# Two-layer hybrid trunk on one core: the delta layer in two phases with a paced MLP filler, and the rotary's sine product read from the PSUM bank

## The chip, the cores and the metric

One core of a Trainium2 chip. The metric is the device time of one launch in microseconds, on the slowest core; there is one core here. The matmuls run on TensorE (PE), elementwise work on VectorE (DVE), ScalarE (ACT) and GpSimd (POOL), and SyncE (SP) issues the DMAs.

## The reference

Two pre-RMSNorm residual layers over an input of 1024 tokens by 1024 channels, each followed by a squared-ReLU MLP of hidden width 4096, and a final RMSNorm:

```python
for layer in range(2):
    hn = rmsnorm(h, mix_norm[layer])
    h = h + (sparse_pool_mixer if layer % 2 == 0 else gated_deltanet)(hn, ...)
    h = h + square(relu(rmsnorm(h, mlp_norm[layer]) @ w_ff1[layer])) @ w_ff2[layer]
return rmsnorm(h, final_norm)
```

The even layer's mixer projects to queries, keys, an indexer and pooling channels. The indexer picks 256 causal keys a query, eight heads attend to them, and a multi-scale pooling branch stands beside. Queries (8 heads of 64 channels) and index queries (8 of 64) get rotary positions: `[x1 cos - x2 sin, x1 sin + x2 cos]` for the two halves of each head. The odd layer's mixer is gated DeltaNet: 8 heads of 128 channels, a short convolution on q, k and v, a decay for each head, and a delta rule whose state passes from chunk to chunk:

```python
v_new = val - kcd @ state
o = qd @ state + at @ v_new
state = state * gl + kd.T @ v_new
```

`val` and `kcd` need the inverse of a unit lower triangular matrix for each chunk. The inverse has no one matmul; it is built level by level.

## The kernel before, in words

The residual stream lives in SBUF in two halves of 512 tokens, `self.h[0]` and `self.h[1]`, each as eight tiles of 128 channels by 512 tokens. All wide matmuls are in split precision: every operand is a high part and a rest, and `mm3` (L245, L246, L247) issues three matmuls of 128x128 by 128x512 for one product. So the three lines always appear in equal number. `split` makes high part (a copy on ScalarE, L165) and rest (a subtraction on POOL, or on VectorE, L169). Weights come by DMA from SP in a prefetch of fixed order (`prefetch`, L200) into a ring `raw` of 4, and go through the same split into the rings W (6) and WM (4).

The odd layer's order is written by generators that the loop in `odd_heads` (L1123) steps in turn:

- `odd_project` projects one of q, k, v, z of a head (24 wide matmuls in bank `ps_g`), copies it out on ScalarE (L947) and convolves on VectorE (L949).
- `odd_head` (L977) is one delta head as a generator of short steps. Small matmuls build the inverse: L1044 and L1050 each issue 16 of 32x32 by 32x16 at every one of four levels (64 a head in the code, which the trace counts as 128); L1037, L1047 and L1053 are VectorE's parts between them. Then the state chain runs over four chunks: L1088 (state times k), L1089 on VectorE, L1090, a copy on ScalarE, L1093 and L1094 for the output, L1097 and L1101 for the new state. L1074 and L1116 stand between the two parts and at the end. Up to three heads are in flight, a new one every `STAGGER` = 8 steps.
- `output` accumulates two finished heads' share of the output projection into h (`accumulate`, L816 to L841).
- The filler is a half of an MLP (`mlp_half`): wide matmuls of known length that depend on nothing in the heads. In every step of the loop it gets a budget in us, `FILL[above]`: 5.6 for the first filler, 4.7 for the second.

The loop runs over all 16 pairs of half and head in one sequence. The first filler is MLP 1 of the second half ("below"). The second ("above") is MLP 2 of the first half; it may start only when the first half's outputs are all written, which is after the second half's first heads have begun:

```python
if not above and fill is None and written[0] == NH // 2:
    fill, due, above = fills[1](), 0.0, True
if fill:
    due += FILL[above]
```

Before the loop, the first half's norm (`norm_stages`, L312: squares, a root on VectorE at L269, transposes at L276 and L288, then the normed x into ring X) and the projections of two heads run beside the filler. After the loop, the rest of the second filler runs beside the second half's last norm, and the last half MLP runs alone ("alone").

In the even layer, `swapped` (L502 to L509) takes a projected pair of heads from bank `ps_g`: a copy on ScalarE into a tile of ring A, and four DMAs on SP that swap the halves of each head (L508). One step later `query_stacks` (L350) calls `rotate` (L334): cosine product on POOL (L339), sine product on VectorE from the swapped copy (L340), sum on VectorE (L341). The keys go through `rotate` with both operands in PSUM. `even_index` and `even_query` are its users: eight times for the index, eight for the queries.

Of the kernel before, what the change touches and what calls it, by code (L numbers as in the profile page):

```python
# [18 lines left out]
OP = mybir.AluOpType  # L19
# [15 lines left out]
FILL = (5.6, 4.7)  # L35
# [89 lines left out]
class Trunk:  # L125
# [224 lines left out]
    def query_stacks(self, p, s, ring):  # L350

        nc = self.nc
        r = self.rotate(*p, s)
# [100 lines left out]
    def even_latent(self, s, ps):  # L454
# [17 lines left out]
        self.kst.append(self.key_stacks(self.rotate(p1, p2, s, True), self.KS))  # L472
# [8 lines left out]
    def even_index_keys(self, s, ps):  # L481
# [9 lines left out]
        self.kis.append(self.key_stacks(self.rotate(p1, p2, s, True), self.KI))  # L491
# [10 lines left out]
    def swapped(self, ps):  # L502

        pc = self.A.get()
        self.copy(pc, ps)
        ps2 = self.A.get()
        for at in range(0, P, 32):
            self.nc.sync.dma_start(ps2[at:at + 32], pc[at ^ 32:(at ^ 32) + 32])  # L508
        return pc, ps2  # L509

    def even_index(self, s, p, ps):

        pc = self.swapped(ps)
# [43 lines left out]
    def even_query(self, s, p, ps):  # L557

        pc = self.swapped(ps)
# [563 lines left out]
    def odd_heads(self, fills):  # L1123


        seq = [(s, h) for s in range(2) for h in range(NH)]
        x, G, qkvz, ys = [[], []], [None, None], {}, {}
        outs, written = deque(), [0, 0]

        def project(i):  # L1130
            s, h = seq[i]
            if h == 0 and s == 1:
                yield from self.norm_stages(self.h[s], R_MIX + 8, x[s])
                yield
            t = []
            for n in range(4):
                while self.live == self.Q.n:
                    yield
                t.append(self.odd_project(s, h, n, x[s]))
                yield  # L1140
                if h == 0 and n == 1:
                    G[s] = self.odd_gates(x[s], self.grow)
                    yield
            qkvz[i] = t
# [8 lines left out]
        def head(i):  # L1153
            s, h = seq[i]
            yield from self.odd_head(s, h, *qkvz.pop(i), G[s], ys)
# [3 lines left out]
        def step(gen):  # L1159
            return next(gen, self) is not self  # L1160

        self.live = 0
        norm = self.norm_stages(self.h[0], R_MIX + 8, x[0])
        ahead, nxt, fill, due, above = None, 2, fills[0](), 0.0, False
        for n in (4, 2, 2):
            next(norm, None)
            for _ in range(n):
                next(fill)
        for _ in chain(project(0), project(1)):
            next(fill)  # L1170
        active, started, done, age = [], 0, 0, 0
        while done < len(seq) or outs:
            if started in qkvz and (not active or (len(active) < 3 and age >= STAGGER)):
                active.append(head(started))
                started, age = started + 1, 0
            age += 1
            for g in list(active):
                if not step(g):
                    active.remove(g)
                    done += 1  # L1180
            for _ in range(2):
                if outs and not step(outs[0]):
                    outs.popleft()
            if not above and fill is None and written[0] == NH // 2:
                fill, due, above = fills[1](), 0.0, True
            if fill:
                due += FILL[above]
                while fill and due > 0:
                    t = next(fill, None)
                    if t is None:  # L1190
                        fill = None
                    else:
                        due -= t
            if ahead is None and nxt < len(seq) and nxt < done + 3:
                if seq[nxt] == (1, 0) and fill:
                    for _ in fill:
                        pass
                    fill = None
                ahead, nxt = project(nxt), nxt + 1
            if ahead and not step(ahead):  # L1200
                ahead = None
# [29 lines left out]
    def even(self):  # L1231
# [3 lines left out]
        with ExitStack() as st:  # L1235
# [3 lines left out]
            self.Q, self.A = Ring(ep, "q", 4, 1024), Ring(ep, "at", 4, 512)  # L1239
# [154 lines left out]
    def run(self):  # L1394
# [10 lines left out]
        XB = Ring(self.pool("second"), "xb", 8, 1024)  # L1405
# [13 lines left out]

        def above():  # L1420
            xa = []
            for _ in self.norm_stages(self.h[0], R_MLP + 8, xa, XB):
                yield FILL[1]
            yield from self.mlp_half(1, 0, xa, [self.Y])

        fill, x = self.odd([below, above]), []
        for _ in self.norm_stages(self.h[1], R_MLP + 8, x):
# [66 lines left out]
```

## Time and profile before

| what | us |
|---|---|
| three runs | 2773.43, 2786.07, 2784.98 |
| their median | 2784.98 |
| the profiled execution's own time | 2783.84 |
| its span in the profile | 2782.1 |
| TensorE busy in it | 2653.8 (95%) |

All readings below are of that one execution. "Granted clock" (PEclk) is the share of TensorE's full 2.4 GHz that it got; 0.5 is its lower level, 1.2 GHz. The stages on the time axis: even layer 0 to 420 (its attention of the second half, and the start of MLP 1, reach beyond it), MLP 1 of the first half to 840, entry of the odd layer 840 to 1000, its heads to 2310, exit to 2450, the last half MLP alone until the end.

### The profile page before, as it was taken

Reading aid. Unit: us, or ns where it says so; the run is one execution under the profiler, and the core shown is the slowest. Engines: PE = TensorE matmul, PEld = TensorE weight load, DVE = VectorE, ACT = ScalarE, POOL = GpSimd, SP = SyncE. Lnnn points to the kernel's source line nnn. Section 1 sums busy time; section 2 is a strip of 40 time slices with the busy share of each in tenths; the row PEclk is TensorE's granted clock in tenths of the full one; section 3 lists DMA queues with packets and bytes.
Section 4 is the critical chain, followed back from the end, with each engine's and each line's share of the span. In section 5 each row is a group of like instructions: output and inputs, shape, how many; then the busy total and the mean of one; then the engine's idle time right before and its main releaser. Section 6 shows DMA issues by size and latency. Waiting matters only on the chain. (4 is left out here: it accounts for less than half of the span.)

```text
span 2782.1 us, 44603 instructions
## 1 busy us (share of the span) xinstructions
PE 2653.8 (95%) x16640; PEld 2094.9 (75%) x16640; DVE 1660.1 (60%) x3587; ACT 1185.8 (43%) x2480; POOL 1227.5 (44%) x1062
## 2 busy tenths in 40 slices
PE   8789989999999999999999999999999999899998
PEld 6566768787777787777777767777777777688886
DVE  5788998734435655655565777655556645633334
ACT  4557767334444543433333344433334333433332
POOL 4653354542245444434454444434444434544442
PEclk9999989999999999999999999999999999999999
DMA  5221223331123222222222212122222222333332
GB/s 192 76 75 35 68 81 98 91 91 54 42 76 96 80 84 73 80 77 78 68 88 73 62 47 64 59 65 77 75 71 73 69 69 87 118 98 95 96 98 76
DMA packets 121068, 220.91 MB, mean 79 GB/s; under 512 B 14098, under 2 KB 15250, under 8 KB 120850
## 3 DMA queue, kind: packets, MB, share of 16 engines
q1 hardware_dynamic: 120850, 218.05, 25.4%
q8 instruction: 131, 2.15, 0.3%
q14 instruction: 87, 0.71, 0.1%
HBM read 209.61 MB, written 4.19 MB: 77 GB/s over the span
## 5 line engine op out<-in xcount | busy, mean ns | idle before, releaser
L169 POOL TENSOR_TENSOR wm<-raw,wm 128x512 fp32r<-128x512 f32 x425 | 562.0, 1323 | 853.9 <-ACT wm L165 840.3
L165 ACT ACTIVATE wm<-raw 128x512 fp32r<-128x512 f32 x425 | 267.3, 629 | 606.2 <-PE ps_g L246 270.7
L169 POOL TENSOR_TENSOR w<-raw,w 128x512 fp32r<-128x512 f32 x222 | 296.7, 1337 | 351.3 <-ACT w L165 330.8
L841 DVE TENSOR_TENSOR h<-ps_d,h 128x512 f32<-128x512 f32 x392 | 267.1, 685 | 134.4 <-PE ps_d L247 132.4
L245 PE MATMUL ps_g<-x,w 128*128 128x512 f32 x644 | 259.5, 403 | 12.1 <-ACT w L165 9.1
L827 DVE SCALAR_TENSOR_TENSOR ps_g<-ps_g,temps 128x512 f32<-128x512 f32 x128 | 89.1, 696 | 291.0 <-ACT temps L825 291.0
L246 PE MATMUL ps_g<-x,w 128*128 128x512 f32 x644 | 257.1, 399 | 4.3 <-DVE x L380 4.1
L247 PE MATMUL ps_g<-x,w 128*128 128x512 f32 x644 | 256.6, 398 | 1.0 <-POOL w L169 1.0
L245 PE MATMUL ps_d<-y,wm 128*128 128x512 f32 x596 | 243.7, 409 | 10.3 <-DVE h L841 8.7
L165 ACT ACTIVATE w<-raw 128x512 fp32r<-128x512 f32 x222 | 139.0, 627 | 258.3 <-PE ps_g L246 180.9
L247 PE MATMUL ps_d<-y,wm 128*128 128x512 f32 x596 | 236.5, 397 | 0.3 <-POOL wm L169 0.2
L246 PE MATMUL ps_d<-y,wm 128*128 128x512 f32 x596 | 236.0, 396 | 0.0
L245 PE MATMUL ps_g<-xb,wm 128*128 128x512 f32 x512 | 207.7, 406 | 5.6 <-ACT qkvz L947 5.0
L247 PE MATMUL ps_g<-xb,wm 128*128 128x512 f32 x512 | 206.4, 403 | 5.5 <-POOL wm L169 5.4
L246 PE MATMUL ps_g<-xb,wm 128*128 128x512 f32 x512 | 205.7, 402 | 0.0
L949 DVE SCALAR_TENSOR_TENSOR qkvz<-temps,conv,qkvz 128x512 f32<-128x512 f32 x144 | 130.8, 909 | 97.9 <-ACT qkvz L947 96.8
L245 PEld LDWEIGHTS ps_g<-x,w 128*128 128x128 f32 x644 | 123.2, 191 | 40.6 <-ACT w L165 9.9
L245 PE MATMUL ps_g<-x,wm 128*128 128x512 f32 x352 | 141.5, 402 | 7.7 <-ACT wm L165 2.9
L246 PEld LDWEIGHTS ps_g<-x,w 128*128 128x128 f32 x644 | 123.0, 191 | 33.3 <-DVE x L380 6.6
L245 PEld LDWEIGHTS ps_d<-y,wm 128*128 128x128 f32 x596 | 112.0, 188 | 44.9 <-DVE h L841 16.9
L246 PE MATMUL ps_g<-x,wm 128*128 128x512 f32 x352 | 140.9, 400 | 4.4 <-DVE x L169 4.4
L247 PE MATMUL ps_g<-x,wm 128*128 128x512 f32 x352 | 141.1, 401 | 3.2 <-POOL wm L169 3.2
(445 smaller groups left out, 6089.5 us busy)
## 6 DMA issues: line engine op xcount, KB each, us to landing
raw<-in_w_dram SPq DMA_DIRECT2D x456, 256.0 KB, 2.7
raw<-in_woi_dram SPq DMA_DIRECT2D x128, 256.0 KB, 2.6
raw<-in_w2q_dram SPq DMA_DIRECT2D x56, 256.0 KB, 2.6
raw<-in_wei_dram SPq DMA_DIRECT2D x52, 256.0 KB, 2.7
raw<-in_weo_dram SPq DMA_DIRECT2D x32, 256.0 KB, 2.7
raw<-in_woo_dram SPq DMA_DIRECT2D x32, 256.0 KB, 2.7
h<-in_xt_dram SPq DMA_DIRECT2D x16, 256.0 KB, 3.0
at<-at SPq DMA_DIRECT2D x64, 64.0 KB, 2.0
```

The source lines that it names most:

```text
L165: self.nc.scalar.activation(out, in_, AF.Copy)
L169: eng.tensor_tensor(lo, full, hi.bitcast(F32), op=OP.subtract)
L245: mm(ps, wh, xh, start=start, stop=False)
L246: mm(ps, wh, xl, start=False, stop=False)
L247: mm(ps, wl, xh, start=False, stop=stop)
L827: nc.vector.scalar_tensor_tensor(ps, ps, 0.0, r, op0=OP.max, op1=OP.mult)
L841: nc.vector.tensor_tensor(h, ps, h, op=OP.add)
L949: nc.vector.scalar_tensor_tensor(acc, pin[:, j:j + 512], cw(j), acc, op0=OP.mult, op1=OP.add)
```

## The change

Two edits. In the odd layer, the sequence of 16 becomes a loop over the halves: each half has its norm, its first projection, its eight heads and its outputs. In every step the filler gets 3.5 us, or 2.8 where a projection is under way. When the first half's outputs are written, the first half's norm for MLP 2 and what is left of the first filler are issued, then MLP 2 of the first half becomes the filler. The normed x of the second half goes to ring XB, that of the first half's MLP 2 to ring X.

In the even layer, `swapped` becomes `rotated`: VectorE multiplies the bank with the sines before the swap, POOL multiplies the copy with the cosines, the DMAs swap the sine product, and one subtraction (L354) ends it. Ring A gets 6 buffers in place of 4. The functions above the change keep their line numbers up to 353; behind, a line's number is higher by 1 to 8 (L340 stays for the keys; L1044 is L1052 now).

```diff
-FILL = (5.6, 4.7)
+FILL = (3.5, 2.8)
...
-    def rotate(self, p, ps2, s, p_in_psum=False):
+    def rotate(self, p, ps2, s):
...
-        (nc.vector if p_in_psum else nc.gpsimd).tensor_tensor(t1, p, cos, op=OP.mult)
+        nc.vector.tensor_tensor(t1, p, cos, op=OP.mult)
...
     def query_stacks(self, p, s, ring):
...
-        r = self.rotate(*p, s)
+        r, m = p
+        nc.vector.tensor_tensor(r, r, m, op=OP.subtract)
...
-    def swapped(self, ps):
-
-        pc = self.A.get()
+    def rotated(self, ps, s):
...
+        pc, pm = self.A.get(), self.A.get()
+        nc.vector.tensor_tensor(pm, ps, sin, op=OP.mult)
         self.copy(pc, ps)
-        ps2 = self.A.get()
+        nc.gpsimd.tensor_tensor(pc, pc, cos, op=OP.mult)
+        m = self.A.get()
         for at in range(0, P, 32):
-            self.nc.sync.dma_start(ps2[at:at + 32], pc[at ^ 32:(at ^ 32) + 32])
-        return pc, ps2
+            nc.sync.dma_start(m[at:at + 32], pm[at ^ 32:(at ^ 32) + 32])
+        return pc, m
...
+        def filled(us):
+
+            self.due += us
+            while self.due > 0:
+                self.due -= next(fill, 1e9)
...
+        for s in range(2):
+            self.due, G = 0.0, {}
+            norm = self.norm_stages(self.h[s], R_MIX + 8, xs[s], (self.X, self.XB)[s])
+            for n in (4, 2, 2):
+                next(norm, None)
+                for _ in range(n):
+                    next(fill)
+            for _ in project(s, 0, G):
                 next(fill)
...
+            active, started, done, age, ahead, nxt = [], 0, 0, 0, None, 1
+            while done < NH or outs:
...
+                filled(FILL[ahead is not None])
+                if ahead is None and nxt < NH and nxt < done + 3:
+                    ahead, nxt = project(s, nxt, G), nxt + 1
+                if ahead and not step(ahead):
+                    ahead = None
+            if s == 0:
+                xa = []
+                norm = self.norm_stages(self.h[0], R_MLP + 8, xa)
+                for _ in range(3):
+                    next(norm, None)
+                    for _ in range(4):
+                        next(fill, None)
+                for _ in fill:
+                    pass
+                fill = fills[1](xa)
...
-            self.Q, self.A = Ring(ep, "q", 4, 1024), Ring(ep, "at", 4, 512)
+            self.Q, self.A = Ring(ep, "q", 4, 1024), Ring(ep, "at", 6, 512)
...
-        for _ in self.norm_stages(self.h[1], R_MLP + 8, x):
+        for _ in self.norm_stages(self.h[1], R_MLP + 8, x, XB):
```

TensorE in the middle of a head of the second half, where before no filler is left. Before (L1088 to L1097 are the state chain of one head, L1044 and L1050 the inverse of the next, L245 to L247 a projection into `ps_g`):

```order
L1088 MATMUL ps_t<-state,qkvz 128x128
L1093 MATMUL ps_o<-state,qkvz 128x128
L1044 MATMUL ps_t<-xxc,lm 32x16 x12
L1090 MATMUL ps_t<-vb,xx_7987 128x128
L1044 MATMUL ps_t<-xxc,lm 32x16 x4
L247 MATMUL ps_g<-x,w 128x512
L245 MATMUL ps_g<-x,w 128x512
L1094 MATMUL ps_o<-vn,at 128x128
L1097 MATMUL ps_t<-vn,kd 128x128
L1050 MATMUL ps_t<-dy,xtc 32x16 x16
L246 MATMUL ps_g<-x,w 128x512
```

After, the same steps of a head (L1096 to L1105, L1052 and L1058 are the same lines of code):

```order
L1096 MATMUL ps_t<-state,qkvz 128x128
L1101 MATMUL ps_o<-state,qkvz 128x128
L1052 MATMUL ps_t<-xxc,lm 32x16 x12
L1098 MATMUL ps_t<-vb,xx_7971 128x128
L1052 MATMUL ps_t<-xxc,lm 32x16 x4
L245 MATMUL ps_d<-y,wm 128x512
L246 MATMUL ps_d<-y,wm 128x512
L1102 MATMUL ps_o<-vn,at 128x128
L1105 MATMUL ps_t<-vn,kd 128x128
L1058 MATMUL ps_t<-dy,xtc 32x16 x16
L247 MATMUL ps_d<-y,wm 128x512
```

The wide matmuls between the chain's steps are as many as before; they come from the filler (`ps_d`, from `y` and `wm`) where they came from a projection.

VectorE in the first half's projections of the even layer, between the index scores (L545 and L547, now L553 and L555; into score tiles named h_...) and the pooling branch (its bank read is L573, now L581). Before:

```order
L547 SCALAR_TENSOR_TENSOR h_606<-ps_t,wi,h_606 128x384
L545 TENSOR_SCALAR h_617<-ps_t,wi 128x512
L547 SCALAR_TENSOR_TENSOR h_617<-ps_t,wi,h_617 128x512
L573 TENSOR_TENSOR temps<-ps_g,rb 128x512
L575 COPY uhist<-temps 128x16
L547 SCALAR_TENSOR_TENSOR h_606<-ps_t,wi,h_606 128x384
L585 SCALAR_TENSOR_TENSOR h_681<-temps 128x512
L547 SCALAR_TENSOR_TENSOR h_606<-ps_t,wi,h_606 128x384
L587 TENSOR_TENSOR h_681<-temps,ce 128x16
L547 SCALAR_TENSOR_TENSOR h_617<-ps_t,wi,h_617 128x512
L588 TENSOR_TENSOR h_681<-h_681,temps 128x16
L340 TENSOR_TENSOR temps<-at,rope 128x512
```

After:

```order
L354 TENSOR_TENSOR at<-at 128x512
L511 TENSOR_TENSOR at<-ps_g,rope 128x512 x2
L553 TENSOR_SCALAR h_610<-ps_t,wi 128x384
L354 TENSOR_TENSOR at<-at 128x512
L555 SCALAR_TENSOR_TENSOR h_610<-ps_t,wi,h_610 128x384
L553 TENSOR_SCALAR h_621<-ps_t,wi 128x512
L555 SCALAR_TENSOR_TENSOR h_621<-ps_t,wi,h_621 128x512
L354 TENSOR_TENSOR at<-at 128x512
L581 TENSOR_TENSOR temps<-ps_g,rb 128x512
L555 SCALAR_TENSOR_TENSOR h_610<-ps_t,wi,h_610 128x384
L583 COPY uhist<-temps 128x16
L593 SCALAR_TENSOR_TENSOR h_681<-temps 128x512
```

The sine product (L340) stood behind the pooling branch's first rows; now the products (L511) stand further ahead, and the last subtraction (L354) stands before the bank read.

SP in the second half's query projections, the last four swaps of the even layer (L508, now L516) among weight loads (L200). Before:

```order
L508 DMA at<-at 32x512 x4
L200 DMA raw<-in_weo_dram 128x512 x2
L508 DMA at<-at 32x512 x4
L200 DMA raw<-in_w_dram 128x512 x2
L508 DMA at<-at 32x512 x4
L200 DMA raw<-in_w_dram 128x512 x2
L508 DMA at<-at 32x512 x4
L200 DMA raw<-in_w_dram 128x512 x4
```

After:

```order
L516 DMA at<-at 32x512 x4
L200 DMA raw<-in_weo_dram 128x512 x2
L516 DMA at<-at 32x512 x4
L200 DMA raw<-in_w_dram 128x512 x3
L516 DMA at<-at 32x512 x4
L200 DMA raw<-in_w_dram 128x512 x2
L516 DMA at<-at 32x512 x4
L200 DMA raw<-in_w_dram 128x512 x3
```

Two or three loads stand between two swaps, where it was two; one more stands ahead of the third.

## Rows read from the trace of the kernel before

**Rows 1.** The page: busy us, share of the span and number of instructions of each engine.

```profile
PE 2653.8 (95%) x16640; PEld 2094.9 (75%) x16640; DVE 1660.1 (60%) x3587; ACT 1185.8 (43%) x2480; POOL 1227.5 (44%) x1062
```

**Rows 2.** The view by stages, all engines: stretch, its length, then busy us and instructions of PE, PEld, DVE, ACT and POOL, granted clock, DMA share, GB/s.

```profile
140.00:420.00 280.00, 248.30 (x1143) 184.37 (x1144) 248.21 (x576) 185.74 (x382) 122.77 (x89) 0.93 0.21 66
...
1540.00:1770.00 230.00, 211.39 (x2032) 160.85 (x2031) 167.24 (x412) 98.97 (x253) 93.40 (x94) 0.95 0.18 54
...
2450.00:2740.00 290.00, 290.00 (x1265) 237.33 (x1264) 102.43 (x157) 95.50 (x158) 134.72 (x104) 1.00 0.32 96
```

**Rows 3.** The same view for line L245 alone, one of the three wide matmul lines: stretch, length, busy us (count), clock, DMA share, GB/s.

```profile
840.00:1000.00 160.00, 85.27 (x214) 0.99 0.28 88
1000.00:1540.00 540.00, 251.27 (x622) 0.99 0.25 77
1540.00:1770.00 230.00, 81.52 (x193) 0.95 0.18 54
1770.00:1860.00 90.00, 39.63 (x97) 0.96 0.23 72
1860.00:2250.00 390.00, 173.35 (x427) 1.00 0.23 71
2250.00:2310.00 60.00, 27.94 (x70) 1.00 0.26 80
2310.00:2450.00 140.00, 71.15 (x182) 1.00 0.33 104
```

**Rows 4.** The same for line L1044, the inverse's matmuls, 128 in the trace for each head.

```profile
1000.00:1540.00 540.00, 11.50 (x768) 0.99 0.25 77
1540.00:1770.00 230.00, 7.97 (x512) 0.95 0.18 54
1770.00:1860.00 90.00, 1.98 (x128) 0.96 0.23 72
1860.00:2250.00 390.00, 9.52 (x608) 1.00 0.23 71
2250.00:2310.00 60.00, 0.44 (x32) 1.00 0.26 80
```

**Rows 5.** TensorE's waits in the exit, 2310 to 2450: who waited, for what, us in total, times, longest.

```profile
PE ps_g L247 <- POOL wm L169: 2.1, 2, 1.5
PE ps_d L245 <- DVE h L841: 2.1, 3, 1.0
...
PE ps_t L276 <- DVE rs_y L269: 1.1, 1, 1.1
```

**Rows 6.** TensorE's waits in 1540 to 1770.

```profile
PE ps_t L276 <- DVE rs_y L269: 4.0, 2, 2.6
PE ps_t L1044 <- DVE xxc L1037: 2.6, 1, 2.6
PE ps_t L1090 <- DVE vb L1089: 2.4, 3, 1.7
PE ps_o L1094 <- ACT vn L165: 2.1, 2, 1.8
```

**Rows 7.** TensorE's waits in 1000 to 1540, the two largest.

```profile
PE ps_g L245 <- ACT qkvz L947: 3.0, 3, 1.0
PE ps_d L245 <- DVE h L841: 2.3, 5, 0.5
```

**Rows 8.** TensorE's waits in the entry, 840 to 1000.

```profile
PE ps_t L276 <- DVE rs_y L269: 2.6, 1, 2.6
```

**Rows 9.** Groups of VectorE by line and form in the even layer, 0 to 420: count, busy us, mean ns, idle before.

```profile
L341 DVE TENSOR_TENSOR temps<-temps 128x512 f32<-128x512 f32 x20 | 19.8, 992 | 0.4
L340 DVE TENSOR_TENSOR temps<-at,rope 128x512 f32<-128x512 f32 x16 | 16.7, 1046 | 9.2 <-DMA at<-at 9.1
...
L340 DVE TENSOR_TENSOR temps<-ps_t,rope 128x512 f32<-128x512 f32 x4 | 2.8, 690 | 1.2 <-PE ps_t L490 1.0 <-PE ps_t L471 0.2
```

**Rows 10.** Line L340 over the whole span: durations in ns, least, median and longest, first and last start.

```profile
L340 DVE TENSOR_TENSOR temps<-at,rope x16: 677/690/1785, 51.4 to 397.0; 128x512 f32<-128x512 f32 x16
L340 DVE TENSOR_TENSOR temps<-ps_t,rope x4: 681/692/693, 42.5 to 175.0; 128x512 f32<-128x512 f32 x4
```

**Rows 11.** The group of the SBUF form of L340 in 140 to 420.

```profile
L340 DVE TENSOR_TENSOR temps<-at,rope 128x512 f32<-128x512 f32 x9 | 9.4, 1046 | 0.0
```

**Rows 12.** TensorE's waits in 350 to 420.

```profile
PE ps_g L246 <- DVE x L169: 4.4, 2, 3.6
PE ps_g L245 <- ACT wm L165: 2.9, 1, 2.9
```

**Rows 13.** The timeline of VectorE from 383 to 392: start, us, line, operation.

```profile
383.40 1.78 DVE L340 TENSOR_TENSOR temps<-at,rope 128x512 f32<-128x512 f32 x1
...
386.81 1.76 DVE L341 TENSOR_TENSOR temps<-temps 128x512 f32<-128x512 f32 x1
388.49 1.76 DVE L340 TENSOR_TENSOR temps<-at,rope 128x512 f32<-128x512 f32 x1
```

**Rows 14.** VectorE's waits in 0 to 140, the first.

```profile
DVE temps L340 <- DMA at<-at: 9.1, 2, 7.8
```

More of the change, by code (lines that the diff above doesn't have):

```diff
@@ L471, in even_latent @@
         nc.tensor.matmul(p2, self.wkv[:, 128:256], cf, start=True, stop=True)
-        self.kst.append(self.key_stacks(self.rotate(p1, p2, s, True), self.KS))
+        self.kst.append(self.key_stacks(self.rotate(p1, p2, s), self.KS))
         pv = self.bank()
@@ L557, in even_query @@
     def even_query(self, s, p, ps):
-        pc = self.swapped(ps)
+        pc = self.rotated(ps, s)
         yield
@@ L1123, in odd_heads, with step @@
     def odd_heads(self, fills):
[L1126 to L1144, printed above, removed]
+        xs, fill = [[], []], fills[0]()
+        qkvz, ys, outs, written = {}, {}, deque(), [0, 0]
+        def step(gen):
+            return next(gen, self) is not self
         def output(s, h):
@@ L1151, in output, with head @@
             written[s] += 1
-        def head(i):
-            s, h = seq[i]
-            yield from self.odd_head(s, h, *qkvz.pop(i), G[s], ys)
+        def head(s, h, G):
+            yield from self.odd_head(s, h, *qkvz.pop(h), G, ys)
             if h % 2:
                 outs.append(output(s, h))
-        def step(gen):
-            return next(gen, self) is not self
-        self.live = 0
-        norm = self.norm_stages(self.h[0], R_MIX + 8, x[0])
-        ahead, nxt, fill, due, above = None, 2, fills[0](), 0.0, False
@@ L1165, in odd_heads @@
-        for n in (4, 2, 2):
-            next(norm, None)
-            for _ in range(n):
-                next(fill)
[L1169 to L1201, printed above, removed]
@@ new lines, in project @@
+        def project(s, h, G):
+            t = []
+            for n in range(4):
+                while self.live == self.Q.n:
+                    yield
+                t.append(self.odd_project(s, h, n, xs[s]))
+                yield
+                if h == 0 and n == 1:
+                    G.update(self.odd_gates(xs[s], self.grow))
+                    yield
+            qkvz[h] = t
+        def filled(us):
+            self.due += us
+            while self.due > 0:
+                self.due -= next(fill, 1e9)
@@ new lines, in odd_heads @@
+        self.live = 0
+        for s in range(2):
[6 more added lines that the diff above has]
+            for _ in project(s, 0, G):
+                next(fill)
+            active, started, done, age, ahead, nxt = [], 0, 0, 0, None, 1
+            while done < NH or outs:
+                if started in qkvz and (not active or (len(active) < 3 and age >= STAGGER)):
+                    active.append(head(s, started, G))
+                    started, age = started + 1, 0
+                age += 1
+                for g in list(active):
+                    if not step(g):
+                        active.remove(g)
+                        done += 1
+                for _ in range(2):
+                    if outs and not step(outs[0]):
+                        outs.popleft()
+                filled(FILL[ahead is not None])
[13 more added lines that the diff above has]
+                fill = fills[1](xa)
@@ L1404, in run @@
         self.banks("odd", self.stack)
-        XB = Ring(self.pool("second"), "xb", 8, 1024)
+        XB = self.XB = Ring(self.pool("second"), "xb", 8, 1024)
         x = []
@@ L1418, in run @@
         below = lambda: self.mlp_half(0, 1, x, [self.Y])
[L1420 to L1424, printed above, removed]
+        above = lambda xa: self.mlp_half(1, 0, xa, [self.Y])
         fill, x = self.odd([below, above]), []
-        for _ in self.norm_stages(self.h[1], R_MLP + 8, x):
+        for _ in self.norm_stages(self.h[1], R_MLP + 8, x, XB):
             for _ in range(4):
```

6 lines of the change are left out of this document (4 added, 2 removed).

## The prediction

> **What bounds the kernel now.** I read the page first. TensorE is busy for 95% of the span and no other engine passes 60% [rows 1]. All of it serves the same matmuls after the change, so the time can move only through what TensorE loses: waits, and stretches at the lower clock. So I cut the trace into stages and asked where it loses [rows 2]. In the dense stretch at 2450 it issues 1265 wide matmuls in 290 us without a gap, 0.229 us each. That price turns every other stage into two parts: wide matmuls times 0.229, and a rest. Wide matmuls come as three lines (L245, L246, L247) in equal number, so their count is three times that of L245 [rows 3]. The rest belongs to the small matmuls of the delta heads, counted by L1044, which each head issues 128 times [rows 4].
>
> - The MLP filler of the first half runs, 1000 to 1540: 1866 x 0.229 = 427.7, rest 112.3 us over 768/128 = 6 heads, **18.7 us a head**.
> - The filler is used up, 1540 to 1770: 579 wide, 132.7, rest 97.3 over 4 heads, **24.3 a head**. TensorE is busy for 211.4 of 230 us and the granted clock averages 0.95: part of the time it was at 1.2 instead of 2.4 GHz.
> - The edge after it, 1770 to 1860: 291 wide, rest 23.3 for 1 head.
> - The second filler runs, 1860 to 2250: 1281 wide, rest 96.4 over 4.75 heads, 20.3 a head.
> - Last head, 2250 to 2310: rest 11.9 with a quarter of a head. Entry, 840 to 1000: rest 12.9. Exit, 2310 to 2450: 546 wide, rest 14.9.
>
> The rests add up to 369.0 us: that is the odd layer's price beyond its wide matmuls. In the even layer the stretch from 140 to 420 is different: VectorE is busy for 248.2 of 280 us there, TensorE for 248.3 at a clock of 0.93 [rows 2].
>
> **The change, part by part: the odd layer.** No matmul is added or removed. The filler goes from 5.6 (first half) and 4.7 us (second) for each step to 3.5, or 2.8 where a projection stands in the step. So it lasts through all eight heads of each half, and the left-over runs densely at the half's end.
>
> *Gone*: the bare stretch and its edge. Above the covered price they held 97.3 - 4 x 18.7 = 22.5 and 23.3 - 18.7 = 4.6, together 27.1 us.
>
> *New*: a second entry (norm of the second half, its gates, one projection before the first head), priced like the first: 12.9. A second drain of the last head: 11.9 less a quarter head is 7.1. A second exit inside the layer: not the whole 14.9, since no result is stored and no weight ring is opened; I count its waits for POOL's weight rest, for VectorE's accumulation and for the norm's root [rows 5], 2.1 + 2.1 + 1.1 = 5 us.
>
> *Unknown*: the price of a head under a filler of about 3.1 us a step, which no stretch shows. From below it is 18.7 (5.6 us of filler). From above I have 20.3 (4.7 us) and the bare stretch: 24.3 less its two waits for the norm's root, 4.0 in all [rows 6], makes 23.3 without filler. A straight line from 20.3 to 23.3 would give 21.3. I take **19.2**, a third of the way from 18.7 to 20.3. The reason is the size of the waits: the bare stretch's longest chain waits are 2.6 (L1044), 1.7 (L1090) and 1.8 us (L1094) [rows 6], and 2.8 to 3.5 us of filler in every step can cover each of them. The order agrees in the short hops: in the place shown, two wide matmuls stand between L1090 and L1094 before and after, only from another source. In the covered stretch the waits are not the chain's at all, but for banks (L947 3.0, L841 2.3) [rows 7]; these stay.
>
> Sum: 16 x 19.2 = 307.2, two entries 25.8, two drains 14.2, the last exit 14.9, the inner exit 5: 367.1 against 369.0, so **-1.9 us**. At 18.7 a head it is -9.9, at 20.3 it is +15.7. The bare stretch's gain is real, but the second entry, drain and exit cost 25 and eat nearly all of it.
>
> The norms: h[0]'s for the second MLP and h[1]'s for the mixer stood in the bare stretch and now stand beside dense filler; the 2.6 us that the first half's norm waits for the root although 18 wide matmuls cover it [rows 8] is in the entry's price. X and XB change owners but every read of the old owner lies before; I cost that at nothing, covered by the eight heads between.
>
> **The even layer.** Sixteen rotaries (eight for the index, eight for the queries). Each had, after the swap by four DMAs, a product on POOL (L339), a product on VectorE (L340), a sum (L341). Now the sine product is read from the bank before the swap, POOL's product stands before it too, and one subtraction is left behind it. VectorE's count stays two, POOL's one, SP's four DMAs.
>
> - The product from SBUF took 1046 ns in the mean, 677 to 1785; the same shape from a bank 690, at most 693 [rows 9, 10]. That is 16 x 0.356 = 5.7 us of VectorE. Nine of them lie in the stretch where VectorE is 89% busy [rows 11], 3.2 us; I count 3 on the path. The remaining subtraction has the sum's form and stays at its 992 ns.
> - At 379 to 391 TensorE waits for the normed x and then for a weight (4.4 and 2.9 us) [rows 12] while VectorE runs two products and a sum of 1.78, 1.78 and 1.76 between and behind the x rests [rows 13]. Of 7.3 us I count 2.
> - New risk: the bank g now waits for VectorE as well as for ScalarE's copy, and the swap's DMAs on SP wait for VectorE; behind them on SP stand weight loads (one more stands ahead of the third swap of the last four, as SP's order shows). And in the place shown the last subtraction stands ahead of the bank read of the pooling branch (L573, now L581), where the product L340 stood eight rows behind it. A product that waited for its swap once held VectorE for 7.8 us [rows 14]. I cost this at nothing while the queues keep that spacing, and at +8 at worst.
>
> So **-5 us**, between -13 (5.7 + 7.3) and +8. By the Trainium skill's page "SBUF — State Buffer" (section Who interferes with whom) a VectorE operation with two SBUF inputs and a POOL operation that reads SBUF exclude each other, and one with a bank as input does not. The trace agrees in the spread of L340 against its bank form. By that rule POOL's side would be freed too, and the even term would rather be -10, the time 2772.
>
> **Sum.** The profiled execution took 2783.8 us, 1.2 below the median 2785.0. 2783.8 - 1.9 - 5 = **2777 us**. About 0.5% is what a measurement of this kernel can tell from no change: faster means below 2771, slower above 2799.
>
> **Rivals.**
> 1. *The cover holds fully.* Heads cost 18.7 and VectorE's relief counts in full: 2783.8 - 9.9 - 13 = 2761. For it: the longest bare wait is below one step's filler. Against it: 20.3 at 4.7 us. Chance 0.30.
> 2. *Thin filler everywhere (slower).* The bare stretch's trouble is spread over all heads: between L1044, L1050 and the state chain L1088 to L1101 TensorE runs dry a little in every step. At 21.3 a head: 16 x 2.1 = +33.6 on the forecast's 19.2, 2777 + 33.6 = 2811. It decides from about 20.6 a head on (16 x 1.4 = +22, to 2799). For it: the line through the three prices. Its second lever is the clock, 0.99 where the filler is thick, 0.95 where it is absent. The Trainium skill's page "TensorE: Matmul & The Clock Gate" (Part 1) holds that the throttled clock is the default and that activity lifts it; by that rule thinning the filler speaks against this change, and the trace agrees as far as 0.95 against 0.99 goes. Chance 0.18.
> 3. *VectorE's queue holds the swap.* The even term turns to +8: 2783.8 - 1.9 + 8 = 2790, no measurable change. Chance 0.08.
> The order shows that the change does what it says, so I keep no chance for that.
>
> **How the numbers follow.** The forecast has 0.44; of it 0.38 within the bound and 0.06 below. Faster 0.30 + 0.06 = 0.36, same 0.38 + 0.08 = 0.46, slower 0.18. The range reaches from 2754 (rival 1 and the spread of the runs, which went 11.6 us below their median) to 2802, where half of rival 2 is left out.
>
> **What would show it.** Right: no stage of 200 us in the odd layer with a clock under 0.97; the rest per head between 18.7 and 20.3 in both halves; a dense stretch without L1044 between the halves; L340's successor at 690 ns throughout. Wrong: a rest above 20.6 a head, with TensorE waiting for L1053, L1089 or L1101 in most steps; new TensorE waits at L245 for the bank-reading product; or an inner exit that costs as much as the last.

## The result and the profile after

The changed kernel takes 2740.66 us in the median of four runs (2736.75 to 2741.31), the kernel before 2779.47 on the same chip: a ratio of 0.9857, 95% interval 0.9838 to 0.9875, 39 us less. The forecast was 2777 and its range ended at 2754. The profiled execution took 2740.07 us (span 2738.3) against 2783.84, 43.8 less; the stages below are those of these two executions, and the one before lies 4.4 us above its median of 2779.47.

The page, as [rows 1]; the instructions are as many, and TensorE is busy for 29 us less:

```profile
PE 2624.8 (96%) x16640; PEld 2078.9 (76%) x16640; DVE 1651.9 (60%) x3587; ACT 1186.8 (43%) x2480; POOL 1226.9 (45%) x1062
```

All matmuls are the same, so I put a shorter busy time down to the clock, and the rest to waits. The clock's own record bears it out: TensorE stood at the lower level for 123 us before and 64 after, and half of the difference is 29.6 us. It is not these two executions alone: over the whole span the granted clock is 0.989 in all four runs of the changed kernel, and 0.977 to 0.983 in the runs of the kernel before that stand beside the experiments. I cut both traces at the same matmul where a stage ends. First before, then after; the even layer and the odd layer (columns: stretch, its length, busy us and count of PE, PEld, DVE, ACT, POOL, granted clock, DMA share, GB/s):

```profile
0.00:510.00 510.00, 451.47 (x1984) 341.54 (x1985) 422.60 (x976) 320.56 (x641) 246.63 (x190) 0.94 0.29 90
840.00:2450.00 1610.00, 1559.70 (x11488) 1230.76 (x11488) 967.86 (x2109) 627.23 (x1434) 716.35 (x672) 0.99 0.25 75
```

```profile
0.00:485.00 485.00, 436.60 (x1984) 335.51 (x1985) 409.14 (x978) 320.09 (x641) 245.23 (x190) 0.97 0.30 94
811.00:2408.00 1597.00, 1548.99 (x11487) 1221.79 (x11486) 976.41 (x2109) 628.50 (x1434) 717.58 (x672) 0.99 0.25 76
```

Even layer: 25 us less, 14.9 of it busy time, 10.1 waits (58.5 to 48.4). Odd layer: 13.0 less, 10.7 of it busy time, 2.3 waits (50.3 to 48.0). The rest of the 43.8 lies in the MLP between them (4.0) and behind the odd layer (1.8). **So two thirds of the gain (29 of 43.8) are TensorE's clock**: the same 1984 matmuls of the even layer keep it busy for 451 us or 437.

The stages of the odd layer after, for L245 alone, as [rows 3]. Heads are counted by L1052 (the old L1044), whose rows follow: the stretches of 427 and 417 us hold six heads each, the two of 83 us the last two of a half:

```profile
811.00:980.00 169.00, 87.25 (x220) 1.00 0.27 85
980.00:1407.00 427.00, 181.40 (x446) 0.99 0.23 70
1407.00:1490.00 83.00, 32.49 (x79) 1.00 0.22 62
1490.00:1640.00 150.00, 78.17 (x198) 1.00 0.29 87
1640.00:1736.00 96.00, 47.90 (x118) 0.98 0.25 79
1736.00:2153.00 417.00, 180.44 (x447) 1.00 0.23 71
2153.00:2236.00 83.00, 32.13 (x78) 1.00 0.20 62
2236.00:2408.00 172.00, 86.63 (x219) 0.98 0.33 100
```

```profile
980.00:1407.00 427.00, 11.54 (x768) 0.99 0.23 70
1490.00:1640.00 150.00, 0.00 (x0) 1.00 0.29 87
1736.00:2153.00 417.00, 11.53 (x768) 1.00 0.23 71
```

With 0.687 us for each L245 (three times 0.229), the rests are 17.9, 120.6, 28.7, 14.0, 14.9, 109.9, 29.4 and 21.5, together 356.9; before they were 369.0. A count of inverses makes the last two heads look a little cheap: the last head's state chain runs in the 150 us behind them, as a row of L1096 (the old L1088) shows (6 of the first half's 48, the other 42 standing in the two stretches of heads):

```profile
1490.00:1640.00 150.00, 1.22 (x6) 1.00 0.29 87
```

A reader sees the new form in these rows: a stretch of 150 us without a single L1052 between the halves, and no stage under a clock of 0.98 where 230 us stood at 0.95.

TensorE's waits after (for what, us in total, times, longest): in the first half's heads, which have the place of [rows 6, 7], then at the inner exit and second entry, then in the last exit, as [rows 5, 8]:

```profile
PE ps_g L247 <- POOL wm L169: 4.3, 4, 3.1
PE ps_d L245 <- DVE h L849: 3.9, 4, 1.6
PE ps_t L1098 <- DVE vb L1097: 2.0, 1, 2.0
```

```profile
PE ps_t L276 <- DVE rs_y L269: 4.0, 1, 4.0
PE ps_d L245 <- DVE h L849: 3.3, 4, 1.3
```

```profile
PE ps_d L245 <- DVE h L849: 2.1, 2, 1.2
PE ps_t L288 <- DVE temps L308: 2.0, 1, 2.0
```

Of the chain waits of the bare stretch (L1044, L1090 and L1094 in [rows 6]) one of 2.0 us is left among the six heads, and two of 1.7 us in all stand at L1058; the two largest items wait for a weight's rest on POOL and for the accumulation on VectorE. The second entry waits 4.0 us for its root, where the one entry before waited 2.6.

The stretch of the even layer that [rows 2] shows, where the clock was 0.93 (the same times, not the same matmuls: 1229 now, 1143 before):

```profile
140.00:420.00 280.00, 256.99 (x1229) 195.01 (x1228) 248.16 (x615) 198.43 (x406) 123.52 (x93) 0.98 0.23 71
```

VectorE's rotary after, as [rows 10] (durations in ns: least, median, longest; the sixteenth product reads another bank and took 677), and its waits for the swap, as [rows 14]:

```profile
L511 DVE TENSOR_TENSOR at<-ps_g,rope x15: 678/685/693, 44.0 to 371.6; 128x512 f32<-128x512 f32 x15
```

```profile
L354 DVE TENSOR_TENSOR at<-at x16: 675/930/1768, 42.5 to 377.9; 128x512 f32<-128x512 f32 x16
...
  DMA at<-at: 3.5, 1
```

The product from the bank never exceeds 693 ns. The subtraction from SBUF still spreads from 675 to 1768. The longest wait for a swap is 3.5 us, where it was 7.8.

### The profile page after: what moved, and what is told of

Its sections match the earlier page's. It is cut to its first block, busy times and chain, and to the rows that moved or that the text cites. A ratio compares the mean times of both kernels' runs of the same rounds, so it can differ in the third digit from the quotient of the medians.

```text
span 2738.3 us, 44618 instructions
## 1 busy us (share of the span) xinstructions
PE 2624.8 (96%) x16640; PEld 2078.9 (76%) x16640; DVE 1651.9 (60%) x3587; ACT 1186.8 (43%) x2480; POOL 1226.9 (45%) x1062
## 4 chain that ended last, share of the span: by engine, by line
PE 53%; DVE 6%; ACT 1%; issue 1%; POOL 0%; DMA 0%; DVEq 0%; ACTq 0%; POOLq 0%
PE ps_g L245 9%; PE ps_g L247 9%; PE ps_g L246 9%; PE ps_d L245 6%; PE ps_d L247 5%; PE ps_d L246 5%; PE ps_t L246 1%; PE ps_t L245 1%; PE ps_t L247 1%; DVE h L849 1%; PE ps_t L1058 1%; PE ps_t L1052 1%; PE ps_o L1102 1%; DVE qkvz L957 1%; PE ps_t L1082 1%
## 5 line engine op out<-in xcount | busy, mean ns | idle before, releaser
L245 PE MATMUL ps_d<-y,wm 128*128 128x512 f32 x596 | 245.4, 412 | 15.5 <-DVE h L849 13.9
L247 PE MATMUL ps_d<-y,wm 128*128 128x512 f32 x596 | 239.8, 402 | 1.9 <-POOL wm L169 1.4
L246 PE MATMUL ps_d<-y,wm 128*128 128x512 f32 x596 | 238.5, 400 | 0.0
L245 PE MATMUL ps_g<-x,wm 128*128 128x512 f32 x476 | 192.0, 403 | 10.1 <-ACT at L165 5.8
L247 PE MATMUL ps_g<-x,wm 128*128 128x512 f32 x476 | 190.6, 400 | 2.9 <-POOL wm L169 2.8
L246 PE MATMUL ps_g<-x,wm 128*128 128x512 f32 x476 | 190.3, 400 | 1.5 <-DVE x L169 1.5
L245 PE MATMUL ps_g<-x,w 128*128 128x512 f32 (+1 forms) x388 | 155.5, 401 | 11.7 <-ACT w L165 9.5
L246 PE MATMUL ps_g<-x,w 128*128 128x512 f32 (+1 forms) x388 | 154.4, 398 | 3.5 <-DVE x L381 2.4
L247 PE MATMUL ps_g<-xb,wm 128*128 128x512 f32 x388 | 153.0, 394 | 4.6 <-POOL wm L169 4.5
L247 PE MATMUL ps_g<-x,w 128*128 128x512 f32 (+1 forms) x388 | 153.1, 395 | 0.0
L245 PE MATMUL ps_g<-xb,wm 128*128 128x512 f32 x388 | 153.1, 394 | 0.0
L246 PE MATMUL ps_g<-xb,wm 128*128 128x512 f32 x388 | 153.0, 394 | 0.0
L245 PEld LDWEIGHTS ps_d<-y,wm 128*128 128x128 f32 x596 | 112.4, 189 | 45.6 <-DVE h L849 16.1
L247 PEld LDWEIGHTS ps_d<-y,wm 128*128 128x128 f32 x596 | 112.3, 188 | 27.1 <-POOL wm L169 3.8
L849 DVE TENSOR_TENSOR h<-ps_t,h 128x512 f32<-128x512 f32 x128 | 88.0, 689 | 69.4 <-PE ps_t L247 69.0
```

The costliest lines, as they stand in the source:

```text
L245: mm(ps, wh, xh, start=start, stop=False)
L246: mm(ps, wh, xl, start=False, stop=False)
L247: mm(ps, wl, xh, start=False, stop=stop)
L849: nc.vector.tensor_tensor(h, ps, h, op=OP.add)
```

## The experiments

Twelve kernels. One table for all: ratio to the kernel before with its interval, then the length in us of the stages between the same wide matmuls (of all those with 512 columns the 1531st, 2651st, 8011th and the last; each profile's own), so that a stage's change can be told from the others'.

| kernel | ratio, interval | even | MLP 1 | odd | last MLP |
|---|---|---|---|---|---|
| before | 1 | 509.6 | 337.5 | 1594.6 | 324.4 |
| changed | 0.9857 (0.9838 to 0.9875) | 484.6 | 333.7 | 1581.9 | 322.3 |
| e1 odd part alone | 0.9939 (0.9924 to 0.9954) | 505.5 | 337.6 | 1578.4 | 322.3 |
| e2 even part alone | 0.9916 (0.9898 to 0.9935) | 485.2 | 333.7 | 1600.3 | 324.4 |
| e3 sine from the copy | 0.9906 (0.9886 to 0.9925) | 497.0 | 336.6 | 1580.0 | 322.3 |
| e4 ring of 4 | 0.9905 (0.9888 to 0.9923) | 497.2 | 334.0 | 1580.1 | 322.3 |
| e5 filler 5.6, 4.7 | 1.0229 (1.0212 to 1.0246) | 492.0 | 332.2 | 1681.4 | 322.3 |
| e6 filler 2.6, 2.0 | 0.9923 (0.9908 to 0.9937) | 487.6 | 333.7 | 1599.6 | 322.3 |
| e7 one sequence, 3.5, 3.2 | 0.9939 (0.9922 to 0.9955) | 484.8 | 333.7 | 1597.2 | 324.4 |
| e8 ring alone | 0.9938 (0.9920 to 0.9957) | 506.0 | 337.3 | 1582.1 | 322.3 |
| e9 longer bank read | 0.9902 (0.9881 to 0.9923) | 493.7 | 339.5 | 1583.5 | 322.3 |
| e10 filler 4.2, 3.4 | 0.9989 (0.9976 to 1.0003) | 487.3 | 333.8 | 1616.4 | 322.3 |
| e11 throwaway matmuls | 1.0198 (1.0177 to 1.0218) | 486.1 | 332.2 | 1675.9 | 322.3 |
| e12 filler 3.8, ring of 7 | 0.9892 (0.9875 to 0.9908) | 487.1 | 333.6 | 1589.6 | 322.3 |

The same even layer appears in eight of them (the changed kernel, e2, e5, e6, e7, e10, e11; e12 but for one buffer) with 484.6 to 492.0 us: that is the spread of one profile's stage. The same odd layer appears in six (the changed kernel, e1, e3, e4, e8, e9) with 1578.4 to 1583.5, and the old one in two, with 1594.6 and 1600.3.

**e1 and e2: each part alone.** The odd layer's hunks of the diff without the even layer's, and the reverse.

> The odd layer's part alone, with the even layer as before. Theory 'two gains that add': of the 43.8 us between the two profiled executions the even layer holds 28 and the odd layer 13, so this run is about 13 us below before, 2766, and its odd layer spends under 20 us at the lower clock where before spent 44. Rival 'the odd part gains only because the even layer no longer ends late (weights further ahead, the topk shorter)': within 4 us of before.

> The even layer's part alone, with the odd layer as before. Theory 'two gains that add': about 26 us below before, 2753, all of it ahead of 520 us on the time axis, half from shorter waits of TensorE (55 to about 42 us of idle time) and half from the clock (58 to about 31 us at the lower level). Rival 'execution to execution the clock of the even layer differs by itself': the low-clock time in 0 to 500 is again above 50 us, and the gain under 15 us.

2762 and 2756 us: 17 and 23 less, 40 together, and the changed kernel has 39. Two gains that add. In e2 the even layer is as short as in the changed kernel, so it is no accident of one profile. Two details missed: e1's odd layer stands at the lower clock for 20.5 us, where under 20 was expected, and e2's gain is 3 us short of its 26. The even part reaches into MLP 1 (333.7 us against 337.5): before, TensorE waits 2.3 us there for the attention's probabilities from VectorE, after it doesn't.

**e3: the sine product from the copy.**

```diff
-        nc.vector.tensor_tensor(pm, ps, sin, op=OP.mult)
         self.copy(pc, ps)
+        nc.vector.tensor_tensor(pm, pc, sin, op=OP.mult)
```

> The changed kernel, with the sine product read from ScalarE's copy in SBUF in place of the bank; it still stands ahead of the swap. Theory 'the bank form pays': 16 products at 1.05 us instead of 0.69 return 5.7 us of VectorE, and with the waits and the clock that hang on them 10 to 20 us come back: 2750 to 2760. Rival 'the order pays' (one operation behind the swap in place of two, and the cosine product out of the way before): at most 4 us come back, 2741 to 2745, although the products are longer.

2754, 13 us back, over half of the even part: the first theory's range, and more than the rival allowed. The products take 1090 ns in the mean instead of 686, and POOL's cosine product, which overwrites the copy, now waits for them. But some 8 to 10 us of the even part's 23 stay, against e1 (2762) and e8 (2764), although the products are as long as in the old rotary: that is what the new order brings together with its ring, in which one operation stands behind the swap where two stood. No run tries the order by itself. VectorE's groups in e3, then POOL's wait:

```profile
L512 DVE TENSOR_TENSOR at<-at,rope 128x512 f32<-128x512 f32 x16 | 17.4, 1090 | 4.6 <-ACT at L165 4.4
L354 DVE TENSOR_TENSOR at<-at 128x512 f32<-128x512 f32 x16 | 17.0, 1062 | 4.1 <-DMA at<-at 4.0
```

```profile
POOL at L513 <- DVE at L512: 9.9, 6, 4.9
```

Two causes are mixed here, the longer time and the place. e9 takes them apart.

**e9: a longer read of the bank, same place.**

```diff
+        nc.vector.tensor_tensor(pm[:, 0:256], ps[:, 0:256], sin[:, 0:256], op=OP.mult)
         nc.vector.tensor_tensor(pm, ps, sin, op=OP.mult)
```

> The changed kernel with half of each sine product done twice: 16 more VectorE operations of 128x256 that read the bank, about 0.37 us each (half of 0.69 and a little), 5.9 us of VectorE in all, ahead of the swap. Theory 'VectorE's time in the projections is the price': as with the product from the copy (5.7 us of VectorE longer, and 13 us came back), 8 to 14 us come back, 2749 to 2755. Rival 'what the copy form cost was its place' (it waits for ScalarE's copy and POOL's product waits for it, 9.9 us in all): the longer read costs 4 us or less, 2739 to 2745.

2753, 12 us back, for 16 operations of 0.42 us (0.37 expected), 6.7 us of VectorE. That is the first theory's range: VectorE time added in the projections costs about twice its length, as in e3 (6.4 us more of it, 13 us of time). The first row below shows the added operations. What the run doesn't separate is VectorE's time from the time that a rotary holds its bank: in one of the sixteen the two reads stand 6 us apart, and TensorE waits 11.2 us for that bank. In this profile the even stage (493.7) is hardly beyond the 492.0 of e5, which has the changed kernel's even layer; the clearer part of the loss stands in MLP 1 (339.5 against 333.7), where TensorE waits 4.5 us for the attention's probabilities, late from VectorE (second row).

```profile
L511 DVE TENSOR_TENSOR at<-ps_g,rope x15: 411/419/426, 48.0 to 378.1; 128x256 f32<-128x256 f32 x15
```

```profile
PE ps_t L246 <- DVE probs L169: 4.5, 1, 4.5
```

**e4 and e8: the ring.** The changed kernel with ring A at 4; and the old rotary, beside the new odd layer, with it at 6.

> The changed kernel with ring A back at 4 buffers. A rotary now holds three tiles (copy, sine product, swapped product) where it held two. Theory 'the ring only keeps it from being worse': the third tile makes the next copy wait for the subtraction, so 3 to 10 us come back, 2744 to 2751. Rival 'the ring is not what binds': 2741, within 3 us. Third, 'the two more buffers are the gain': 20 us or more come back.

> The odd layer as changed, the even layer's rotary as before with ring A at 6 buffers instead of 4. The odd part alone with 4 gave 2762. Theory 'the old rotary holds two tiles and does not need the ring': within 3 us of 2762. Rival 'the ring is a gain by itself, since the next copy waits for the sine product': 2750 to 2757.

With 4 buffers 12 us come back, more than the first theory's 10 and less than the third's 20. The old rotary gains nothing by 6 (2764 against 2762). The third tile of the new rotary needs them: in e4 the bank's product waits until the subtraction's readers have freed a tile.

```profile
DVE at L511 <- POOL y L361: 9.1, 2, 5.2
```

The even layers of e3, e4 and e9 in this order, in the row form of above, the changed kernel's being 485 us with 436.60 busy:

```profile
0.00:497.00 497.00, 439.65 (x1983) 337.04 (x1984) 418.31 (x976) 318.85 (x640) 247.47 (x189) 0.96 0.29 92
```

```profile
0.00:497.00 497.00, 443.82 (x1982) 339.61 (x1983) 408.62 (x978) 319.46 (x640) 244.99 (x189) 0.95 0.29 92
```

```profile
0.00:494.00 494.00, 438.68 (x1984) 335.63 (x1985) 419.97 (x993) 320.61 (x641) 247.08 (x190) 0.96 0.30 92
```

In these single profiles e3 and e9 give the time back mostly as waits (57.4 and 55.3 against 48.4), e4 more as clock (443.8 busy against 436.6).

**e5, e6, e10: the filler's pace.** `FILL` at (5.6, 4.7), (2.6, 2.0) and (4.2, 3.4), nothing else.

> The changed kernel with FILL back at (5.6, 4.7): two phases, but the filler is used up before the last heads of each half. Theory 'the pace keeps the clock': the last two heads of each half run bare, the time at the lower clock in the odd layer goes from 17 back to 35 to 50 us, and 8 to 15 us come back: 2749 to 2756. Rival 'the structure pays' (no second half's heads waiting for the first half's outputs): within 4 us of 2741.

> The changed kernel with FILL at (2.6, 2.0): a quarter less filler in each step, and a longer dense rest behind each half. Theory 'what counts is that no step is bare': the waits grow by a few us (47 to 52 of idle time in the odd layer), the clock stays: 2741 to 2748. Rival 'there is a threshold': the chain's waits of 1.7 to 2.6 us come through in most steps and the clock falls with them, 20 us or more: 2761 and above.

> The changed kernel with FILL at (4.2, 3.4), between 3.5, where 150 us of filler are left at the end of the first half, and 5.6, where it is used up before the last head. Some 75 steps with 0.6 us more take about 47 us of the 135 that are left, so it still lasts. Theory 'it only has to last': 2737 to 2745. Rival 'each step's cover pays': a head costs 1 us less, 16 us in all, 2725. Third, 'the price grows with the pace' (20.4 us a head at 5.6, 19.2 at 3.5): 2746 to 2752.

None came as expected. e5 loses 104 us against the changed kernel, ten times what I expected: the direction of its first theory, not its size. Its first six heads cost 20.3 us each, hardly more than 20.1, and those of the second half 20.2 against 18.3: some 13 us in all. The rest, over 80 us, is lost at the two ends, where the filler is used up while the last head is still under way and the norm and the next entry follow. Rows of e5, the heads 0 to 5 and the two ends:

```profile
997.00:1515.00 518.00, 502.52 (x3971) 398.39 (x3958) 291.73 (x665) 190.81 (x453) 225.05 (x227) 0.99 0.24 74
1590.00:1655.00 65.00, 45.66 (x372) 33.58 (x370) 29.84 (x82) 13.04 (x38) 8.00 (x11) 0.65 0.07 21
2385.00:2455.00 70.00, 49.65 (x450) 36.99 (x442) 32.36 (x89) 15.29 (x43) 13.24 (x14) 0.67 0.11 34
```

In 65 us TensorE is busy for 46 at a clock of 0.65. Of the 99.5 us that e5's odd layer is longer than the changed kernel's, 40.7 are busy time of the same matmuls and 58.8 are waits. e10 shows the same in small. Its heads are the cheapest of all (18.5 and 18.8 us), yet it is 35 us slower: between the last head's last matmul (L1124) and the second half's norm (its last L276) stand only 312 wide matmuls, where the changed kernel has 504, and the exit at 2285 to 2444 runs dry on its root, its norm and its last MLP rows.

```profile
1540.00:1758.00 218.00, 201.30 (x902) 156.37 (x900) 130.21 (x225) 92.55 (x180) 102.18 (x81) 0.96 0.25 78
2285.00:2444.00 159.00, 138.60 (x687) 108.59 (x687) 88.95 (x157) 55.41 (x104) 66.39 (x55) 0.92 0.28 88
```

```profile
PE ps_d L245 <- ACT y L834: 6.3, 1, 6.3
PE ps_t L276 <- DVE rs_y L269: 4.3, 2, 2.5
PE ps_t L288 <- DVE temps L308: 3.4, 1, 3.4
```

In e6 the ends are covered, but the heads are thinner: in 769 us of its middle heads the clock averages 0.98 (41 us at the lower level in the odd layer, 17 in the changed kernel), and its odd layer is 18 us longer. By the account of wide matmuls and rests the heads hold 8 of these; the other 10 lie in entries, middle and exit, and I have no cause for them.

**e7: the thin pace in one sequence.** The changed even layer, the old loop, `FILL = (3.5, 3.2)`.

> The even layer as changed, the odd layer's loop as before (one sequence of 16 heads), with the filler at (3.5, 3.2) instead of (5.6, 4.7). The even layer's part alone with the old pace gave 2756. Theory 'the bare stretch belongs to the one sequence': the second filler still has to wait for the first half's last outputs, so a bare stretch of two to three heads stays, with 30 us or more at the lower clock: 2748 to 2756. Rival 'the pace alone does it': the two phases are not needed, 2738 to 2745.

2762, 6 us more than the old pace in e2 and 21 more than the two phases. The odd layer in the row form of above, before at 1559.70 busy of 1610:

```profile
812.00:2424.00 1612.00, 1550.91 (x11486) 1225.56 (x11485) 970.71 (x2109) 626.62 (x1434) 716.03 (x671) 0.99 0.25 75
```

The thin pace alone gives the busy time of the changed kernel (1550.9), so it keeps the clock; and it pays with waits, 61 us instead of 48. The phases at the old pace (e5) are worse than nothing. Each needs the other.

**e11: more work, no more time.** e5 with six wide matmuls (`nc_mm` is `nc.tensor.matmul`) a step into a spare bank, once the filler is used up. They compute nothing that is used.

```diff
-                self.due -= next(fill, 1e9)
+                t = next(fill, None)
+                if t is None:
+                    self.due, ps = 0.0, self.bank("d")
+                    for n in range(6):
+                        nc_mm(ps, xs[s][0][:, 0:P], xs[s][n][:, 0:512], start=n == 0, stop=n == 5)
+                    return
+                self.due -= t
```

> The thick filler again (5.6, 4.7; 2845 us), and where it is used up each step issues six wide matmuls into a spare bank that nothing reads: 14 times in each half, 168 matmuls, 38 us of work more for TensorE at the full clock. Theory 'the bare end is slow because the clock falls': the time at the lower clock in the two ends goes from 123 us to under 40, which gives back over 40 us, and with the waits that the matmuls fill the kernel gets faster by 10 to 40 us for doing more: 2805 to 2835. Rival 'the bare end is slow because its chain waits': the matmuls cost what they don't hide in 28 us of idle time a half: 2845 to 2865.

There are 216 of them, not 168: 49 us of work. The kernel takes 10 us **less** (2834 against 2845). Of that only 5.5 us stand in the odd layer (1675.9 against 1681.4); 5.9 stand in the even layer, which the edit doesn't touch, and belong to the spread. So the sure reading is that 49 us of added work cost nothing. Its two last heads, against those of e5 shown above:

```profile
1585.00:1650.00 65.00, 58.98 (x486) 44.07 (x484) 32.64 (x88) 14.75 (x41) 8.77 (x12) 0.97 0.07 21
2380.00:2450.00 70.00, 63.71 (x534) 47.66 (x534) 36.31 (x93) 18.20 (x47) 14.22 (x16) 0.96 0.10 31
```

The clock is 0.97 and 0.96 where it was 0.65 and 0.67, and in the whole odd layer the time at the lower level goes from 140 to 55 us, the waits from 106 to 75. The bare end is slow for both reasons. The waits give back 31 us. The clock gives back some 24: TensorE's busy time rises by 25.5 us (1575.4 to 1601.0) for 49.5 us of added work. Half of the 85 us at the lower level would be more, but that counts idle time with it: in a third of e5's 140 us TensorE isn't busy.

**e12: between.** `FILL = (3.8, 3.1)` and ring A at 7.

> The changed kernel with FILL at (3.8, 3.1) and ring A at 7, two edits in stages that do not touch each other (the two parts' gains added up to the whole), so each is read from its own stage. At 3.5 the twelve first heads cost 19.2 us each and the ends after them 53 us beyond their wide matmuls; at 4.2 the heads cost 18.7 and the ends 84. Theory 'the ends need some 500 wide matmuls': at 3.8 the rest is still long enough, the heads get some 4 us cheaper in all, odd layer 1576 to 1584. Rival 'the optimum is at 3.5 and narrow': odd layer 1590 or more. Ring A, 7: if two rotaries in flight are enough, the even layer stays at 485 within 2 us; if the third one waits for a tile, it falls by 4 or more. Together 2733 to 2742, or 2750.

2749. The odd layer is 8 us longer than at 3.5: the ends are covered, but the second half's heads cost 20.0 instead of 18.3 (six heads and 460 L245 in 436 us, second row). That is neither theory's number, though close to the rival's. The even layer shows no gain from a seventh buffer (487). The changed kernel stays the fastest of the thirteen.

```profile
984.00:1420.00 436.00, 187.07 (x460) 0.99 0.22 71
1740.00:2176.00 436.00, 187.84 (x460) 0.99 0.22 70
```

## Why the prediction was wrong

- **The even term failed, by about 18 us.** I put it at -5, at most -13; e2 measured -23. The counts were right: a product of 1046 ns became one of 686, and 16 of them are 5.7 us. The step that failed was "I count 3 on the path". It treated VectorE's microseconds as worth one each at most, and only in one stretch. e9 priced them: 6.7 us of VectorE are 12 us of time, and e3 takes back 13. The other 8 to 10 us stay in e3: they come with the new order and its ring, which I had only as a risk, at nothing, and at +8 at worst. In this stage a late VectorE leaves TensorE waiting; 14.9 of the profile's 25 us, though, are busy time. I had read the clock of 0.93 in [rows 2] and gave it no price at all. Why the clock rose in the even layer stays open: e3 and e9 bring back only 3.0 and 2.1 us of the busy time, e4 7.2, and no run here forced waits and clock apart.
- **Ring A** I did not price. It is no gain by itself (e8), and without it half of the even part is gone (e4).
- **VectorE's queue holds the swap** (third rival, +8): it did not. The one wait for a swap that the subtraction has is 3.5 us. By the Trainium skill's rule that I set beside the sum (page "SBUF — State Buffer", section Who interferes with whom), POOL should be freed as well: its cosine product went from 1522 to 1366 ns in the mean, 2.5 us in all, so the trace agrees in sign. But most of that isn't shown to be the rule's: in e3, whose sine product has both inputs in SBUF again, POOL's product takes 1412 ns, and in e9, with the bank as input, 1405. The -10 worked out beside that rule was nearer than my own -5 and still too small.
- **The odd term was too small, by 10 to 15 us.** Forecast -1.9; by the same account the one profile gives -12.1, and e1 measured -17. The price of a head held: I took 19.2 us, and the twelve heads with a successor cost (120.6 + 109.9) / 12 = 19.2. What failed is that I charged all sixteen at it: the last two heads of each half, behind the last projection, have rests of 28.7 and 29.4 us, about 14.5 a head. Since part of their chain runs in the stretches behind, heads, drains and exits are best taken together: 341.3 charged, 324.1 measured. The entries cost more than forecast, 32.8 instead of 25.8.
- **The reason for 19.2 was wrong.** I drew a line from 18.7 (5.6 us of filler) over 20.3 to 23.3 (none), as though a thicker filler made a cheaper head. At paces of 2.6, 3.5, 3.8, 4.2 and 5.6 in the same structure the middle heads cost 19.7, 19.2, 20.0, 18.7 and 20.3: no slope. These differences are not noise: in the six kernels with the changed odd layer the first half's heads cost 19.8 to 20.3 and the second's 18.2 to 18.4. Why the halves differ stays open. My 23.3 was dear in good part because of the clock, and I counted it as chain: 0.05 of 230 us is 11.5 us, 2.9 for each of the four heads.
- **Thin filler everywhere** (second rival, +34) has a weak trace at a thinner pace: at 2.6 (e6) the heads cost 8 us more in all. At 3.5 it does not set in; the busy time of the odd layer fell. The page "TensorE: Matmul & The Clock Gate" (Part 1) of the Trainium skill holds that activity lifts the clock. The trace agrees (e11: 0.65 to 0.97 with added matmuls; e6: 41 us at the lower level against 17). But I took from it only that thinning the filler speaks against the change, and did not ask whether any stretch is left bare, which costs far more (e5).
- **The cover holds fully** (first rival, 2761) was nearest in number, and still 20 us short, since it too left the clock out.
- **Base and range.** The forecast started from 2783.8, 4.3 us above the median that the result is set against. The range's lower end of 2754 is not the sum that it names either: 2761 less 11.6 is 2749, still above the measured time.

Of the signs by which I wanted to know it, these came: no long stage under 0.97, the dense stretch between the halves, the bank form at 690 ns throughout. The heads cost 20.1 and 18.3, the second below the 18.7 that I had named as the least. The inner exit's stretch has a rest of 14.0, near the last exit's 14.9 before, which I had named as a sign of being wrong; but it holds the last head's drain, and with the drain's 7.1 I had charged 12.1 for it.

## What to carry to other kernels

Where one engine is busy for 95%, split its loss into waits and busy time before you cost a change: the same matmuls that take longer are the clock, and it needs a price of its own in the forecast. Take the busy time for it, not the time at the lower level, since part of that can be idle (a third in e5's odd layer). Filler work that waits for nothing is worth most where nothing else is left, at the ends of a phase: pace it so that a rest survives there, and measure a few paces, since here too thick a pace (e5, +104 us) is far dearer than too thin a one (e6, +19). And a new temporary needs its buffers in the same edit (e4).

## What the runs showed that I had not expected

- 216 matmuls whose result nobody reads, 49 us of work, cost a kernel no time: in two stretches of 65 and 70 us the granted clock rose from 0.65 and 0.67 to 0.97 and 0.96.
- 6.7 us of VectorE in a stage where it is busy for about 85% cost 12 us, part of it behind the stage, where attention's probabilities come late.
- The price of a head does not follow the pace of the filler: 18.7 at 4.2 us stands between 20.0 at 3.8 and 20.3 at 5.6.
